# A scaled copy of 16,384 tokens for two experts each: the later weights move from SyncE's DMA queue to ScalarE's

## The chip, the cores and the metric

The kernel runs on one NeuronCore of a Trainium2 chip. Time is the device time of one execution in microseconds (us). VectorE (DVE in the profile) and ScalarE (ACT) compute; SyncE (SP) and ScalarE issue the DMA transfers, each to a queue of its own (q1 for SyncE, q10 for ScalarE), and 16 DMA engines of the core carry them out. TensorE and GpSimd take no part in the work.

## What is computed

```python
x               # 16 x 1024 x 512, float32
expert_weights  # 16 x 1024 x 2, float32
x_expanded = x[:, :, np.newaxis, :].repeat(2, axis=2)
weights = expert_weights[..., np.newaxis]
return (x_expanded * weights).astype(np.float32)
```

Each token's row of 512 numbers is written twice, once times each of its two weights. 33.6 MB are read and 67.1 MB are written. The indices of the experts are not used.

## The kernel before

The 16,384 tokens are 128 partitions times 128 tokens. They are cut into five tiles of 25 tokens on every partition (`groups`) and a rest of 3 (`LAST`). In each tile a partition's tokens lie next to each other in memory, so a load or a store moves one run of bytes for each partition: 25 tokens of x are a run of 51,200 bytes.

Three kinds of buffers stand in on-chip memory. `w_tile` holds all weights. `x_pool` has two buffers for a tile's x, so that tile i + 2 can be loaded when tile i has been used (line 164). `o_ring` holds the products of one tile, 25 tokens of 1,024 numbers, and every tile writes into the same places; the place of a piece is free again when its store has landed. The last 3 tokens have a small buffer of their own for x, `z_tile`.

A tile is worked on in pieces (`CUTS`): tile 0 in tokens 0 to 2, 2 to 13 and 13 to 25, the others in 0 to 13 and 13 to 25. `fill` (line 145) gives the first tokens of a piece to VectorE, in instructions of up to 4 tokens (line 130), and the others to ScalarE, one instruction of 512 numbers for each token and weight (line 120). After each piece `emit` has SyncE issue its store (line 155). The text calls the store of tile i's piece j "store i.j".

The loads of x are issued by ScalarE (line 80), tile 0's in three steps of 2, 7 and 16 tokens (`FIRST`). Loading tile 2 also brings the last tokens' x (line 87); a copy of one element (line 77) goes ahead of it.

The weights are issued by SyncE. Tile 0's are issued right after the first step of its load (line 85). The others come in three transfers, `later_weights` (line 101): tiles 1 and 2, tiles 3 and 4, and the last 3 tokens. The first two have, for each partition and tile, a run of 50 numbers, 200 bytes; the third a run of 24 bytes. They are issued once store 0.0 has been (line 157). What puts them there is the copy of line 102, a VectorE copy from `o_ring` into the part of `w_tile` that they fill: it comes after the first product, and the transfers have to come after it.

Each engine carries out its own instructions in their order, and so does each queue. The order between engines is kept by semaphores that the framework adds. An engine that issues transfers also waits at times, before an issue, for an earlier transfer that counts on the same semaphore.

Of the kernel before, what the change touches and what calls it, by code (L numbers as in the profile page):

```python
# [1 line left out]

# [4 lines left out]


@with_exitstack
def kernel(  # L10
    ctx: ExitStack,
    tc: tile.TileContext,
    x: bass.AP,
    expert_indices: bass.AP,
    expert_weights: bass.AP,
    out: bass.AP,
):
    nc = tc.nc

    batch, seq, hidden = x.shape  # L20
    k = expert_weights.shape[-1]
    P = nc.NUM_PARTITIONS
    ntok = batch * seq
    assert ntok % P == 0
    A_TOTAL = ntok // P

    f32 = mybir.dt.float32
    row = k * hidden
    CH = 4


    groups = [25, 25, 25, 25, 25]
    TX = max(groups)
    LAST = 3
    FIRST = [2, 7, 16]
    CUTS = [[0, 2, 13, 25], [0, 13, 25]]
    SHARES = [[2, 7, 9], [8, 8]]
    assert sum(groups) + LAST == A_TOTAL

    xf = x.rearrange("b s h -> (b s) h")  # L40
    of = out.rearrange("b s k h -> (b s) (k h)")
    wf = expert_weights.rearrange("b s k -> (b s) k")

    w_pool = ctx.enter_context(tc.tile_pool(name="w_pool", bufs=1))
    x_pool = ctx.enter_context(tc.tile_pool(name="x_pool", bufs=2))
    o_pool = ctx.enter_context(tc.tile_pool(name="o_pool", bufs=1))

    w_tile = w_pool.tile([P, A_TOTAL * k], f32)
    o_ring = o_pool.tile([P, TX * row], f32)

    def rows(of_all, done, T):
        return of_all[done * P : (done + T) * P, :].rearrange(
            "(p a) n -> p (a n)", a=T
        )


    if LAST:
        z_pool = ctx.enter_context(tc.tile_pool(name="z_pool", bufs=1))
        z_tile = z_pool.tile([P, LAST * hidden], f32)

    tiles = []
    done = 0
    for n in groups:
        tiles.append((done, n))
        done += n

    loaded = []

    def load(i):
        if i >= len(tiles):  # L70
            return
        done, n = tiles[i]
        x_tile = x_pool.tile([P, TX * hidden], f32)
        src = rows(xf, done, n)
        steps = FIRST if i == 0 else [n]
        if i == 2 and LAST:
            nc.scalar.copy(out=z_tile[:, :1], in_=o_ring[:, TX * row - 1 :])  # L77
        for e, step in enumerate(steps):
            at = sum(steps[:e])
            nc.scalar.dma_start(  # L80
                out=x_tile[:, at * hidden : (at + step) * hidden],
                in_=src[:, at * hidden : (at + step) * hidden],
            )
            if i == 0 and e == 0:
                weights(0, T0)
        if i == 2 and LAST:
            nc.scalar.dma_start(out=z_tile, in_=rows(xf, A_TOTAL - LAST, LAST))
        loaded.append(x_tile)


    T0 = groups[0]
    head = len(tiles) * T0

    def weights(at, to):
        g = (to - at) // T0
        nc.sync.dma_start(
            out=w_tile[:, at * k : to * k].rearrange("p (g n) -> p g n", g=g),
            in_=wf[at * P : to * P, :].rearrange("(g p a) n -> p g (a n)", g=g, p=P),
        )

    def later_weights():
        nc.vector.tensor_copy(  # L102
            out=w_tile[:, T0 * k :], in_=o_ring[:, : (A_TOTAL - T0) * k]
        )
        weights(T0, 3 * T0)
        weights(3 * T0, head)
        nc.sync.dma_start(
            out=w_tile[:, head * k :], in_=rows(wf, head, A_TOTAL - head)
        )

    def product(engine, o_tile, t, x_in, c, m):

        o = t * row
        if engine is not None:
            for e in range(m * k):
                out_e = o_tile[:, o + e * hidden : o + (e + 1) * hidden]
                in_e = x_in[:, e // k * hidden : (e // k + 1) * hidden]
                w_e = w_tile[:, c + e : c + e + 1]
                if engine is nc.scalar or engine is nc.any and (c + e) % 3 == 2:
                    nc.scalar.mul(out=out_e, in_=in_e, mul=w_e)  # L120
                else:
                    nc.vector.tensor_scalar(
                        out=out_e,
                        in0=in_e,
                        scalar1=w_e,
                        scalar2=None,
                        op0=mybir.AluOpType.mult,
                    )
            return
        nc.vector.tensor_tensor(  # L130
            out=o_tile[:, o : o + m * row].rearrange(
                "p (t k h) -> p t k h", t=m, k=k
            ),
            in0=x_in[:, : m * hidden]
            .rearrange("p (t h) -> p t h", t=m)
            .unsqueeze(2)
            .to_broadcast([P, m, k, hidden]),
            in1=w_tile[:, c : c + m * k]
            .rearrange("p (t k) -> p t k", t=m)
            .unsqueeze(3)  # L140
            .to_broadcast([P, m, k, hidden]),
            op=mybir.AluOpType.mult,
        )

    def fill(o_tile, x_in, c, m, v):
        for t in range(0, v, CH):
            u = min(t + CH, v)
            product(None, o_tile, t, x_in[:, t * hidden : u * hidden], c + t * k, u - t)
        product(nc.scalar, o_tile, v, x_in[:, v * hidden :], c + v * k, m - v)

    def emit(src, dst, c, cuts, shares):
        for at, to, v in zip(cuts, cuts[1:], shares):
            o_tile = o_ring[:, at * row : to * row]
            fill(o_tile, src[:, at * hidden : to * hidden], c + at * k, to - at, v)
            nc.sync.dma_start(out=dst[:, at * row : to * row], in_=o_tile)  # L155
            if c == 0 and at == 0:
                later_weights()

    for i in range(2):
        load(i)  # L160
    for i, (done, n) in enumerate(tiles):
        form = min(i, 1)
        emit(loaded[i], rows(of, done, n), done * k, CUTS[form], SHARES[form])
        load(i + 2)
    emit(
        z_tile,
        rows(of, A_TOTAL - LAST, LAST),
        (A_TOTAL - LAST) * k,
        [0, LAST],
        [LAST],  # L170
    )

# [1 line left out]
_INS = ['x', 'expert_indices', 'expert_weights']  # L174
_OUTS = [((16, 1024, 2, 512), 'float32')]


# [23 lines left out]
```

## Time and profile before

| | |
|---|---|
| median of 3 runs | 240.14 us (239.68 to 240.2) |
| the profiled execution, its time | 239.99 us |
| its span in the profile | 238.2 us |
| VectorE busy | 93.6 us, 24 instructions |
| ScalarE busy | 55.1 us, 88 instructions |
| moved by the DMA engines | 100.80 MB, 423 GB/s over the span |

In the profile's rows L130 is line 130 of the kernel; "out<-in" names the buffer that is written and the one that is read; x3 is a count of instructions. SPq and ACTq are the issues of DMAs by SyncE and ScalarE. A row of the timeline has the start and the time from the first to the end of the last of its instructions, in us, and in brackets how long the engine was idle before it and what ended that. A row of DMA issues has the size of one transfer and the us from its issue to its landing. A row of a DMA queue has the number of its packets, MB, and the time that they took as a share of 16 engines' time in the stretch. A row of stretches has the stretch in us from the start and its length, the busy us of VectorE, ScalarE and GpSimd with their instructions, the clock, the DMA engines' share and their GB/s. The line of digits divides the span into 40 slices of about 6 us; 9 is a share of 90% or more.

### The profile page before, as it was taken

The page shows a single profiled execution, that of the slowest core. Times are in us where ns is not written, and L with a number is a line of the kernel's source. Part 1 is how long each engine was busy: PE and PEld are TensorE (multiplying, and loading weights), DVE is VectorE, ACT ScalarE, POOL GpSimd, SP SyncE. Part 2 cuts the span into 40 slices and gives each one's busy share as a digit, 9 for nine tenths or more (in the row PEclk, how much of TensorE's full clock was granted, in tenths as well). Part 3 has the DMA queues.
Part 4 walks back from the last instruction along what each step waited for, and adds up shares of the span by engine and source line. Part 5 has one row for each costly group of instructions (what it writes and reads, how often), then busy time and mean ns, then how long its engine had stood idle before and what let it go on. Part 6 is the DMA issues. An engine that isn't in the chain of part 4 may idle for free.

```text
span 238.2 us, 213 instructions
## 1 busy us (share of the span) xinstructions
DVE 93.6 (39%) x24; ACT 55.1 (23%) x88; POOL 0.2 (0%) x4
## 2 busy tenths in 40 slices
DVE  2774910000068292095005902910085292861300
ACT  0004920000063260090005202700080280800000
POOL 0000000000000000000000000000000000000000
DMA  7999999998999999999999999999999999999996
GB/s 261 423 437 435 414 466 484 432 378 386 484 396 396 532 438 425 424 404 406 403 484 443 447 433 416 405 412 473 447 429 438 416 396 486 429 429 444 413 398 262
DMA packets 3713, 100.80 MB, mean 423 GB/s; under 512 B 1152, under 2 KB 1152, under 8 KB 1408
## 3 DMA queue, kind: packets, MB, share of 16 engines
q1 hardware_dynamic: 2560, 67.24, 65.4%
q10 hardware_dynamic: 1152, 33.55, 33.2%
q14 instruction: 1, 0.01, 0.0%
HBM read 33.69 MB, written 67.11 MB: 423 GB/s over the span
## 4 chain that ended last, share of the span: by engine, by line
DMA 53%; issue 20%; DVE 17%; ACT 3%; ACTq 0%; DVEq 0%; SPq 0%
DMA out_dram<-o_ring 45%; DVE o_ring L130 17%; DMA x_tile<-in_x_dram 8%; ACT o_ring L120 2%; ACT L120 1%; ACTq L80 0%; DVEq L130 0%; SPq L155 0%; ACTq L120 0%
## 5 line engine op out<-in xcount | busy, mean ns | idle before, releaser
L130 DVE TENSOR_TENSOR o_ring<-x_tile,w_tile 128x4096 f32<-128x4096 f32 (+3 forms) x22 | 90.0, 4131 | 122.1 <-DMA out_dram<-o_ring 64.0
L120 ACT ACTIVATE o_ring<-x_tile,w_tile 128x512 f32<-128x512 f32 x86 | 53.7, 708 | 132.5 <-DMA out_dram<-o_ring 132.5
L120 ACT ACT_TABLE_LOAD x1 | 1.3, 1283 | 20.9 <-DMA x_tile<-in_x_dram 20.9
L130 DVE TENSOR_TENSOR o_ring<-z_tile,w_tile 128x3072 f32<-128x3072 f32 x1 | 3.4, 3360 | 7.0 <-DMA out_dram<-o_ring 7.0
L102 DVE COPY w_tile<-o_ring 128x206 f32<-128x206 f32 x1 | 0.3, 269 | 0.0
L77 ACT COPY z_tile<-o_ring 128x1 f32<-128x1 f32 x1 | 0.2, 192 | 0.0
L185 POOL MEMSET const-bfloat16-1.0<- 128x1 bf16 x1 | 0.1, 102 | 0.0
L185 POOL MEMSET const-uint8-127<- 128x1 uint8 x1 | 0.1, 102 | 0.0
L185 POOL MEMSET const-float32-0.0<- 128x1 f32 x1 | 0.1, 99 | 0.2 <-issue 0.2
L185 POOL MEMSET const-float32-1.0<- 128x1 f32 x1 | 0.1, 99 | 0.0
## 6 DMA issues: line engine op xcount, KB each, us to landing
out_dram<-o_ring SPq DMA_DIRECT2D x5, 6144.0 KB, 36.7
out_dram<-o_ring SPq DMA_DIRECT2D x4, 6656.0 KB, 29.0
x_tile<-in_x_dram ACTq DMA_DIRECT2D x4, 6400.0 KB, 33.1
out_dram<-o_ring SPq DMA_DIRECT2D x1, 5632.0 KB, 40.2
x_tile<-in_x_dram ACTq DMA_DIRECT2D x1, 4096.0 KB, 19.2
x_tile<-in_x_dram ACTq DMA_DIRECT2D x1, 1792.0 KB, 7.8
out_dram<-o_ring SPq DMA_DIRECT2D x1, 1536.0 KB, 14.6
out_dram<-o_ring SPq DMA_DIRECT2D x1, 1024.0 KB, 17.9
```

Source lines behind the costliest of these rows:

```text
L77: nc.scalar.copy(out=z_tile[:, :1], in_=o_ring[:, TX * row - 1 :])
L102: nc.vector.tensor_copy(out=w_tile[:, T0 * k :], in_=o_ring[:, : (A_TOTAL - T0) * k])
L120: nc.scalar.mul(out=out_e, in_=in_e, mul=w_e)
L130: nc.vector.tensor_tensor(out=o_tile[:, o : o + m * row].rearrange("p (t k h) -> p t k h", t=m, k=k), in0=x_in[:, : m * hidden] .rearrange ...
L185: nc = _bacc.Bacc("TRN2", target_bir_lowering=False, num_devices=1)
```

## The change

The issuing engine becomes an argument of `weights`. `later_weights` is called while tile 0 is loaded, after its three steps and before the load of tile 1, and its three transfers are issued by ScalarE. The copy into `w_tile` is gone, and with it the call after store 0.0. On ScalarE the three issues stand between the third load of tile 0 and the load of tile 1; on SyncE store 0.1 follows store 0.0 directly. The waits of all other instructions name the same semaphores as before.

```diff
--- before.py
+++ after.py
@@ -82,7 +82,9 @@
                 in_=src[:, at * hidden : (at + step) * hidden],
             )
             if i == 0 and e == 0:
-                weights(0, T0)
+                weights(nc.sync, 0, T0)
+        if i == 0:
+            later_weights()
         if i == 2 and LAST:
             nc.scalar.dma_start(out=z_tile, in_=rows(xf, A_TOTAL - LAST, LAST))
         loaded.append(x_tile)
@@ -91,20 +93,17 @@
     T0 = groups[0]
     head = len(tiles) * T0
 
-    def weights(at, to):
+    def weights(engine, at, to):
         g = (to - at) // T0
-        nc.sync.dma_start(
+        engine.dma_start(
             out=w_tile[:, at * k : to * k].rearrange("p (g n) -> p g n", g=g),
             in_=wf[at * P : to * P, :].rearrange("(g p a) n -> p g (a n)", g=g, p=P),
         )
 
     def later_weights():
-        nc.vector.tensor_copy(
-            out=w_tile[:, T0 * k :], in_=o_ring[:, : (A_TOTAL - T0) * k]
-        )
-        weights(T0, 3 * T0)
-        weights(3 * T0, head)
-        nc.sync.dma_start(
+        weights(nc.scalar, T0, 3 * T0)
+        weights(nc.scalar, 3 * T0, head)
+        nc.scalar.dma_start(
             out=w_tile[:, head * k :], in_=rows(wf, head, A_TOTAL - head)
         )
 
@@ -153,8 +152,6 @@
             o_tile = o_ring[:, at * row : to * row]
             fill(o_tile, src[:, at * hidden : to * hidden], c + at * k, to - at, v)
             nc.sync.dma_start(out=dst[:, at * row : to * row], in_=o_tile)
-            if c == 0 and at == 0:
-                later_weights()
 
     for i in range(2):
         load(i)
```

## The prediction

> **What bounds the kernel now.** I read the page first, then the chain that ended last, then the timeline of the first 100 us, and last the DMA queues in single stretches. Three parts of the page say the same thing:
>
> ```profile
> span 238.2 us, 213 instructions
> DVE 93.6 (39%) x24; ACT 55.1 (23%) x88; POOL 0.2 (0%) x4
> DMA  7999999998999999999999999999999999999996
> ...
> q1 hardware_dynamic: 2560, 67.24, 65.4%
> q10 hardware_dynamic: 1152, 33.55, 33.2%
> ```
>
> No compute engine is busy for half of the span, and the 16 DMA engines are at 80% or more in all slices but the first and the last. q1 carries SyncE's transfers (all stores, all weights), q10 ScalarE's (all x). Together their packets take 98.6% of the span, 0.986 x 238.2 = 234.9 us of each DMA engine. So 3.3 us are all the idle time there is. The chain shows where some of it lies:
>
> ```profile
> 1.65 19.21 DMA x_tile<-in_x_dram
> ...
> 198.00 21.23 DMA out_dram<-o_ring
> ...
> 219.35 3.36 DVE o_ring L130
> ```
>
> Data first moves at 1.65 us. The last product ends at 219.35 + 3.36 = 222.71, and its store, in the issue rows below, lands 14.6 us later, at 237.3; 0.9 us of the span follow. Take 1.65 and 0.9 from 3.3, and 0.75 us of DMA idle time is left, ramps at both ends among it. That is the hard fact of this case: a reordering of transfers can win no more than this, plus what it makes the packets themselves cheaper.
>
> Now the stretch that the change touches:
>
> ```profile
> out_dram<-o_ring SPq DMA_DIRECT2D x1, 5632.0 KB, 40.2
> x_tile<-in_x_dram ACTq DMA_DIRECT2D x1, 512.0 KB, 3.9
> out_dram<-o_ring SPq DMA_DIRECT2D x1, 1536.0 KB, 14.6
> w_tile<-in_expert_weights_dram SPq DMA_DIRECT2D x2, 50.0 KB, 45.4
> w_tile<-in_expert_weights_dram SPq DMA_DIRECT2D x1, 25.0 KB, 2.7
> out_dram<-o_ring SPq DMA_DIRECT2D x1, 1024.0 KB, 17.9
> ```
>
> ```profile
> 0.72 4.30 ACTq L80 DMA_DIRECT2D x_tile<-in_x_dram  x4
> 7.02 0.27 DVE L102 COPY w_tile<-o_ring 128x206 f32<-128x206 f32 x1
> 7.41 1.02 SPq L96 DMA_DIRECT2D w_tile<-in_expert_weights_dram  x2
> 8.47 0.49 SPq L107 DMA_DIRECT2D w_tile<-in_expert_weights_dram  x1
> 8.96 7.69 DVE L130 TENSOR_TENSOR o_ring<-x_tile,w_tile 128x4096 f32<-128x4096 f32 x2 [1.68 <-DMA x_tile<-in_x_dram]
> 20.88 9.90 DVE L130 TENSOR_TENSOR o_ring<-x_tile,w_tile 128x4096 f32<-128x4096 f32 x3 [4.22 <-DMA x_tile<-in_x_dram]
> 27.27 4.02 SPq L155 DMA_DIRECT2D out_dram<-o_ring  x2
> 31.01 0.35 ACTq L80 DMA_DIRECT2D x_tile<-in_x_dram  x1
> 67.62 8.76 DVE L130 TENSOR_TENSOR o_ring<-x_tile,w_tile 128x4096 f32<-128x4096 f32 x2 [36.84 <-issue]
> 82.06 8.76 DVE L130 TENSOR_TENSOR o_ring<-x_tile,w_tile 128x4096 f32<-128x4096 f32 x2 [5.67 <-DMA out_dram<-o_ring]
> 90.90 0.36 ACTq L80 DMA_DIRECT2D x_tile<-in_x_dram  x1
> ```
>
> The later weights are issued from 7.41 and land some 45 us later, near 54. The second store (tile 0, tokens 2 to 13; I call it store 0.1) is issued at 27.27 behind them and lands at 27.27 + 40.2 = 67.5, when VectorE, after 36.84 us of waiting, may overwrite that part of the ring. The DMA queues of 22 to 50 us show why, and the two stretches after it what came of it:
>
> ```profile
> DMA packets 512, 12.37 MB, mean 442 GB/s; under 512 B 268, under 2 KB 268, under 8 KB 268
> q10 hardware_dynamic: 256, 12.29, 101.3%
> q1 hardware_dynamic: 256, 0.08, 1.1%
> ...
> DMA packets 628, 1.57 MB, mean 391 GB/s; under 512 B 484, under 2 KB 484, under 8 KB 612
> ...
> DMA packets 368, 16.58 MB, mean 436 GB/s; under 512 B 32, under 2 KB 32, under 8 KB 32
> ```
>
> 256 packets against 256: the two queues take turns packet by packet, and a 200-byte row of weights waits for a 51,200-byte row of x each time. The stores are indeed held. But the engines moved 442 GB/s meanwhile, nearly all of it x: tiles 1 and 2 were loaded ahead, and between 56 and 94 us (third row) the stores had the engines to themselves at 436. The hold changed the order of the bytes, not their rate. Only 50 to 54 us (second row), with 484 small packets, falls to 391: against the 439 around it a loss of 4 x (1 - 391/439) = 0.44 us.
>
> **The change, part by part.** The sum starts from the profiled execution's own 239.99 us; the median of the runs is 240.14.
>
> *The copy goes.* 0.27 us of VectorE at 7.02, in front of a product that then waited 1.68 us more for x. Cost and gain 0; without that cover 0.27.
>
> *Three issues leave SyncE's queue.* 1.02 + 0.49 = 1.51 us. The next instruction there is store 0.1, which isn't issued before 27.27 because ScalarE's products come late: 0. The Trainium skill speaks against more: "DMA: Bandwidth & Descriptors", section "Issuing engines are not separate DMA queues", has the DMAs of all issuing engines interleave on the same 16 DMA engines, so that another issuer saves sequencer time alone. By that rule the time stays 239.99; the 442 GB/s of the held stretch agree.
>
> *The same three issues enter ScalarE's queue* ahead of tile 1's load. The four loads' row reaches from 0.72 to 5.02, while the first load lands at 0.72 + 3.9 = 4.62, so I read the fourth issue as waiting for that landing. Three loads at about 0.4 us each end near 2, three weights near 3.5: inside that wait, 0. If the cover failed, tile 1's load would be queued 1.5 us later, near 6.2, still some 14 us before q10 has finished tile 0 at 20.88. ScalarE's products behind it wait for that landing too, so nothing behind it is held.
>
> *The rows of the weights change queue.* The three transfers make 256 + 256 + 128 rows, 48 small packets on each engine with the completions set aside. They now run in one go after tile 0's last load, from about 20.5 us, with the rest of the first store beside them. If the 0.44 us at 50 to 54 simply vanishes, -0.44. If every one of some 800 small packets pays what the 484 paid, 0.44 x 800/484 = 0.73, less the 0.44 already paid: +0.3. I take the middle, -0.1.
>
> *Loads and stores now mix.* Store 0.1, no longer held, takes turns with tiles 1 and 2. The smallest load took 3.9 us from issue to landing, so I allow some 3 to its first byte: it starts near 30. Tile 1's load has by then had 9 us at 442 GB/s, 4 MB; of the 13.1 MB of both tiles 9.1 remain, and some 8 MB of stores run beside them. Mixed stretches exist, tile 3's load at 96 to 124 us and tile 4's at 142 to 170, to be held against stores alone at 172 to 230:
>
> ```profile
> q1 hardware_dynamic: 140, 6.14, 50.7%
> q10 hardware_dynamic: 128, 5.94, 49.7%
> ...
> q1 hardware_dynamic: 140, 6.14, 50.6%
> q10 hardware_dynamic: 128, 5.99, 49.9%
> ...
> q1 hardware_dynamic: 554, 25.27, 100.6%
> ...
> 96.00:124.00 28.00, 8.76 (x2) 6.24 (x10) 0.00 (x0) 1.00 1.00 432
> 142.00:170.00 28.00, 8.76 (x2) 6.24 (x10) 0.00 (x0) 1.00 1.01 433
> 172.00:230.00 58.00, 29.64 (x7) 16.25 (x26) 0.00 (x0) 1.00 1.01 436
> ```
>
> Mixed, a MB takes 1.004 x 28 x 16 / 12.08 = 37.2 and 1.005 x 28 x 16 / 12.13 = 37.1 engine-microseconds; stores alone 1.006 x 58 x 16 / 25.27 = 36.9, x alone (22 to 50 us) 1.013 x 28 x 16 / 12.29 = 36.9. So mixing costs about 0.25 per MB: 17 MB x 0.25 / 16 = +0.27 us. By the rates in the last column (432.5 against 439) it would be 17 MB, 39.3 less 38.7 us, +0.6; but one row of 51,200 bytes on 16 engines is 0.8 MB, and a stretch's edge moves its rate by more than that difference. The low end is 0. I take +0.25.
>
> *Where the stall goes.* While alternating, store 0.1 has 45,056 of each 96,256 bytes, 47% of 432 = 203 GB/s: 5.77 MB take 28 us, landing near 58. VectorE starts tile 1 about 59 instead of 67.62 and issues its store near 68. In front of that store lies store 0.2, and when that lands the same bytes have moved as before (tile 0 to 2, weights, the first three stores, but for some rows of the last tokens): near 82 again. The next product starts where it started, at 82.06, tile 3's load at 90.90, and from there the old order repeats. So 8 us won at 59 become 14 us of slack (68 to 82) ahead of a full queue: 0 at the end. If a queue of stores ran dry here, each us of it would count fully.
>
> Sum: -0.1 + 0.25 = +0.15, 239.99 + 0.15 = **240.1 us**. With the ends -0.44 and +0.9 its own range is 239.6 to 240.9.
>
> **The rivals.** *Slower: the weights stand alone at the head of q10.* Near 21 us the first store is nearly through (issued after the first product, at 7.0, it landed 17.9 us later), and store 0.1 comes only at 27.27. If 48 small rows on each engine can't be streamed, nothing covers the gap before tile 1's rows. Its price goes up to one uncovered transfer: the first weights landed 2.7 us after their issue began, 0.37 of it issue time by the row below, so 2.3 us. It decides from about 0.5 us of gap. Halfway between the +0.3 above and 2.3 gives +1.3, 241.3 us.
>
> ```profile
> 0.73 0.37 SPq L96 DMA_DIRECT2D w_tile<-in_expert_weights_dram  x1
> ```
>
> For it: the dip at 50 to 54. Against it: 391 GB/s are no standstill, and x rows of tile 1 are queued right behind. The Trainium skill has a price for this: "DMA: Bandwidth & Descriptors", section "Measured (HBM→SBUF, 128 partitions, SWDGE, issued from GpSimd)", gives 0.95 us for 64 KB and 0.68 us for 4 KB, an estimate of 2.6 us for the three and 242.6 in all if none of it is covered; the trace's 0.44 us for most of these rows is far below it. Chance 0.28, a double price of mixing among it.
>
> *Faster: the earlier start reaches the end.* If the 0.75 us of unexplained idle time sit in the middle and vanish with the held stores, 239.2; with the whole 0.44 as well, 238.8. For it: tile 1 does start sooner. Against it: no slice between the second and the last but one is below 8 tenths. Chance 0.22.
>
> *The change doesn't do what it says:* stores could wait for x rows in turn whatever the weights do, store 0.1 landing near 67 again. Then the bytes are the same too, and the time is 240.0. 0.05, without a change of time.
>
> **How the numbers follow.** A measurement here tells 0.2%, about 0.48 us, from no change. The forecast has 0.45 and the ineffective change 0.05, both inside that: same 0.50, slower 0.28, faster 0.22. The range reaches to the slower rival's 241.3 and the faster one's 239.2, leaving their far ends out: 239.2 to 241.4.
>
> **What would show it.** Right: store 0.1 lands at 55 to 62 us instead of 67.5; VectorE's products at 82 and tile 3's load at 91 stay within 1 us; the DMA slices stay at 9; weights land near 22. Wrong: a slice at 20 to 30 us below 9 tenths (the slower rival); tile 3's load sooner than 89 (the faster one); a mean rate of 30 to 70 us below 430 GB/s (mixing dearer than taken).

## The result and the profile after

The changed kernel takes 240.93 us in the median of 22 runs (239.68 to 242.64), against 239.89 us (239.53 to 240.93) for the kernel before. The ratio is 1.005, with a 95% interval of 1.0036 to 1.0065: slower by some 1.1 us (1.04 between the medians, 1.2 by the ratio), where no change was the likeliest forecast. Two more samplings of 12 runs each gave 1.0044 (1.0017 to 1.0072) and 1.0045 (1.0028 to 1.0062). The runs also spread more widely than before. One execution further down, of e10, took 243.97 us and counts as a slow run, so that e10's ratio leaves it out.

From the page of the changed kernel, whose profiled execution took 241.64 us:

```profile
span 239.9 us, 212 instructions
DVE 93.3 (39%) x23; ACT 55.1 (23%) x88; POOL 0.2 (0%) x4
DMA  6999999999999999999999999999999999999983
...
q1 hardware_dynamic: 1872, 67.14, 64.8%
q10 hardware_dynamic: 1840, 33.66, 33.2%
...
out_dram<-o_ring SPq DMA_DIRECT2D x1, 5632.0 KB, 32.0
```

The rows of the moved weights are now in q10's count. The packets take 64.8 + 33.2 = 98.0% of the span, 0.980 x 239.9 = 235.1 us of each DMA engine: as much as before (234.9). No slice in the middle has a hole. What is new is the last slice, 3 tenths instead of 6, after one of 8. Here are the last microseconds in finer slices of 0.25 us, 230 to 240 us, first of before, then of after:

```profile
DMA  0499944017496969699996945110000000000000
GB/s 0 197 1376 393 786 197 197 0 49 295 197 492 295 590 295 541 295 492 442 393 541 295 541 197 246 49 49 0 0 0 0 0 0 0 0 0 0 0 0 0
```

```profile
DMA  9994490089989594969999432212020110000000
GB/s 393 1376 590 197 197 393 0 0 344 442 393 344 639 246 541 197 492 295 492 393 492 492 197 148 98 98 49 98 0 98 0 49 49 0 0 0 0 0 0 0
```

Both keep up the full rate to about 235.7 us. Before, the last data starts at 236.6. After, it goes on at 49 to 98 GB/s until 238.2, and 49 GB/s in a slice is one 12,288-byte row: a few engines, at the end one alone, still have work when the others have none. The timeline of after shows what the start of the changed region did, and where the time was lost:

```profile
2.12 1.54 ACTq L98 DMA_DIRECT2D w_tile<-in_expert_weights_dram  x2
3.70 0.50 ACTq L106 DMA_DIRECT2D w_tile<-in_expert_weights_dram  x1
4.96 0.35 ACTq L80 DMA_DIRECT2D x_tile<-in_x_dram  x1
...
59.85 8.76 DVE L129 TENSOR_TENSOR o_ring<-x_tile,w_tile 128x4096 f32<-128x4096 f32 x2 [28.71 <-issue]
...
81.46 8.76 DVE L129 TENSOR_TENSOR o_ring<-x_tile,w_tile 128x4096 f32<-128x4096 f32 x2 [12.85 <-DMA out_dram<-o_ring]
90.29 0.36 ACTq L80 DMA_DIRECT2D x_tile<-in_x_dram  x1
...
128.99 8.76 DVE L129 TENSOR_TENSOR o_ring<-x_tile,w_tile 128x4096 f32<-128x4096 f32 x2 [17.05 <-DMA out_dram<-o_ring]
...
175.08 8.76 DVE L129 TENSOR_TENSOR o_ring<-x_tile,w_tile 128x4096 f32<-128x4096 f32 x2 [17.84 <-DMA out_dram<-o_ring]
...
221.02 3.36 DVE L129 TENSOR_TENSOR o_ring<-z_tile,w_tile 128x3072 f32<-128x3072 f32 x1 [6.96 <-DMA out_dram<-o_ring]
```

The last four of the corresponding products stood in before at:

```profile
82.06 8.76 DVE L130 TENSOR_TENSOR o_ring<-x_tile,w_tile 128x4096 f32<-128x4096 f32 x2 [5.67 <-DMA out_dram<-o_ring]
...
127.83 8.76 DVE L130 TENSOR_TENSOR o_ring<-x_tile,w_tile 128x4096 f32<-128x4096 f32 x2 [17.55 <-DMA out_dram<-o_ring]
...
173.42 8.76 DVE L130 TENSOR_TENSOR o_ring<-x_tile,w_tile 128x4096 f32<-128x4096 f32 x2 [17.42 <-DMA out_dram<-o_ring]
...
219.35 3.36 DVE L130 TENSOR_TENSOR o_ring<-z_tile,w_tile 128x3072 f32<-128x3072 f32 x1 [6.97 <-DMA out_dram<-o_ring]
```

After is 0.60 us ahead at 82 us (some rows of the last tokens' x are still to come then), 1.16 behind at 129, 1.66 behind at 175, and 1.67 at the end. Each of these products waits for a store, and a store has landed when the slowest of the 16 engines has written its part. So the loss arises while tile 3's and tile 4's loads run beside the stores, 60 us and more behind the place of the change, and in single engines, since their mean did not move.

**One engine out of step.** The trace lists every DMA packet. It does not name the engine, but on one engine a row starts 3 to 4 ns ahead of the recorded end of the row before it, so that an engine can be followed row by row. The stretch in which store 0.1's first rows come in, of after first, then of its third sampling (e8 below); q10 carries x, q1 this store, with packets, MB and the packets' time as a share of the stretch on 16 engines:

```profile
DMA packets 16, 0.81 MB, mean 542 GB/s; under 512 B 0, under 2 KB 0, under 8 KB 0
q10 hardware_dynamic: 15, 0.77, 123.6%
q1 hardware_dynamic: 1, 0.05, 6.9%
```

The same stretch of the third sampling:

```profile
q10 hardware_dynamic: 15, 0.77, 147.9%
q1 hardware_dynamic: 1, 0.05, 6.9%
```

One turn of the 16 engines (30.4 to 31.9 and 30.1 to 31.6 us): 15 take a row of tile 1's x, and one takes the store's first row. From there that engine takes a store row when the others take x, and the other way round. In the second sampling (e2) it was 13 and 3. The store was issued at 27.2 to 27.6 and its rows were there some 3.4 us later, just while the engines were ending their rows of x (30.2 to 31.1): some ended a moment too early for the store, one or a few late enough. Then tile 3's load begins. The first rows of it that start after 95.2 us in after, and after 95.85 in e8:

```profile
q10 hardware_dynamic: 1, 0.05, 14.2%
```

```profile
q10 hardware_dynamic: 1, 0.05, 30.6%
```

One packet each, of 51,200 bytes on one engine, 0.142 x 16 x 1.4 us = 3.18 us and 0.306 x 16 x 0.75 = 3.67 us long, where such a row takes 1.89. The other 15 engines had begun theirs between 94.7 and 95.2, and this one came 0.6 to 0.7 us later. In e2 it took 2.6 us. Nothing behind that place levels it: from 172 us on, when there are only stores, the engines' distances stay the same within some 0.15 us.

Followed to the end, the engine out of step is the last one in e8: it finishes its rows at 238.7 us and the other 15 by 236.3. In e2 three engines finish at 236.6 to 237.4 and the others by 236.2. In the first profile of after, however, the engine with the row of 3.18 us finishes at 237.9 and is only the last but one. The last, at 238.7, had been in step near 30 us and near 95; it lost 2.6 us during tile 4's load, where its rows of x took 2.77, 2.11, 2.12, 2.50 and 2.59 us between 144 and 168 us. The first of them stands alone in the window of 144.275 to 144.3 us, 6.922 x 16 x 0.025 us long:

```profile
q10 hardware_dynamic: 1, 0.05, 692.2%
```

The product at 175 us waited for this engine, which finished that store's rows at 174.6 us, so the half microsecond that after loses between 129 and 175 us is its doing; being out of step at tile 1 does not explain it. In before, too, the last engine (lag 0.7 in the table below) had three rows of x of 2.2 to 2.3 us in the loads of tiles 3 and 4. So the loss is that of single engines in all three profiles of after, but not in each by the same step.

An accounting of the profiles bears out that the last engine sets the span. "Packets" is the sum of all packets' times divided by 16; "lag" is how far the last engine's completion of the last store is behind the mean of the 16; both are worked out from the trace's records.

| profile | span | packets | lag | rest |
|---|---|---|---|---|
| before | 238.2 | 235.2 | 0.7 | 2.2 |
| e1, before again | 238.2 | 235.1 | 0.9 | 2.2 |
| after | 239.9 | 235.1 | 2.4 | 2.3 |
| e2, after again | 238.5 | 235.2 | 1.2 | 2.2 |
| e8, after again | 239.8 | 235.1 | 2.5 | 2.2 |
| e12, store 0.1 0.7 us sooner | 237.6 | 234.9 | 0.3 | 2.4 |

In these rows the rest stays within 0.2 us, and the difference in span between the first and the third row, 1.7 us, is the difference in lag.

### The profile page after: what moved, and what is told of

The parts are those of the page before. It is cut to its first block, busy times and chain, and to the rows that moved or that the text cites. A ratio compares the mean times of both kernels' runs of the same rounds, so it can differ in the third digit from the quotient of the medians.

```text
span 239.9 us, 212 instructions
## 1 busy us (share of the span) xinstructions
DVE 93.3 (39%) x23; ACT 55.1 (23%) x88; POOL 0.2 (0%) x4
## 2 busy tenths in 40 slices
DMA packets 3713, 100.80 MB, mean 420 GB/s; under 512 B 1152, under 2 KB 1152, under 8 KB 1408
## 3 DMA queue, kind: packets, MB, share of 16 engines
q1 hardware_dynamic: 1872, 67.14, 64.8%
q10 hardware_dynamic: 1840, 33.66, 33.2%
## 4 chain that ended last, share of the span: by engine, by line
DMA 57%; issue 17%; DVE 17%; ACT 3%; ACTq 0%; DVEq 0%; SPq 0%
DMA out_dram<-o_ring 49%; DVE o_ring L129 17%; DMA x_tile<-in_x_dram 8%; ACT o_ring L119 2%; ACT L119 1%; ACTq L80 0%; DVEq L129 0%; SPq L154 0%; ACTq L119 0%
```

## The experiments

Thirteen runs were made, each timed in five rounds against the kernel before. The expectations call the theories by letters, which came up in this order: S, the spread of the engines at the end, arising from order; N, one bad draw; A, the weights' issues on ScalarE's queue; F, the freed stores as such; L, a load that joins the stores while all engines stand in step; O, one engine out of step.

**Is it repeatable? (e1, e2, e8: the two kernels unchanged)**

> The kernel before once more, as the measure of what repeats. All theories: ratio 1.000 +- 0.002. Theory S (spread of the DMA engines at the end): its profile again has the DMA engines running out within about 1.2 us of each other at the end (before: the share falls from 236.0 and is gone at 237.0), and its times stay within 239.5 to 241. Theory N (the profile of after shows one bad draw that either kernel could have had): its tail would be now and then as long as after's 3 us, its runs spread as widely as after's 239.7 to 242.6.

> The changed kernel once more. S: ratio 1.004 to 1.007 (about 241), runs spread over 2 to 3 us, the tail of the profile longer than 1.2 us whenever its run is above 240.5. N: 1.000 to 1.003 with a tail like before's. Theory A (ScalarE's issues of the weights near 2 us delay the start): the first product starts at 4.9 to 5.0 again instead of 4.69.

> The changed kernel a third time, for a third profile of the spread: F and L both want span = 2.3 us + mean packet time of an engine + how far the last engine is behind the mean, within 0.2 us, whatever the draw; ratio 1.003 to 1.007.

e1: 1.0004 (0.9987 to 1.0021). e2: 1.0044, its first product at 4.29 us, sooner than before's 4.69, so that the late start in the first profile of after (4.96) was a draw and A loses its first half. e8: 1.0045. N falls: the loss came three times out of three, while its size varies within a kernel's runs (e2's went from 239.09 to 242.37), as the accounting has it.

**The stores freed in two other ways (e3, e5)**

```diff
-        if i == 0:
+        if i == 1:
             later_weights()
```

> The weights stay on ScalarE's queue, but are issued after tile 1's load: the start is as in before (ScalarE issues nothing but x until 4.6 us), while the stores are free as in after. S: nothing gained, 1.003 to 1.007 (about 241). A: 1.000 to 1.002 (240.0), first product at 4.7, weights near 36 us without harm.

e3: median 240.18, ratio 1.0036 (1.0019 to 1.0053); S has it in its band, and A wanted 1.002 at most. The lag was 0.2 us, but the packets took 235.8 us. Its rows of x took 2.6 to 2.9 us instead of 1.89 on all 16 engines at the one turn, near 30 us, at which store 0.1 joined, about 0.8 us of each engine. The weights, now behind tile 1's x, landed so late that tile 1's products waited for them until 65.8 us. What that cost is not separated out; rows of x between 76 and 80 us were longer, too, by 0.3 us of each engine.

```diff
-        weights(nc.scalar, T0, 3 * T0)
-        weights(nc.scalar, 3 * T0, head)
-        nc.scalar.dma_start(
+        weights(nc.gpsimd, T0, 3 * T0)
+        weights(nc.gpsimd, 3 * T0, head)
+        nc.gpsimd.dma_start(
```

> The three later weight transfers go to GpSimd's own queue: the stores are as free as in after, and ScalarE's queue is as in before. Theory F (the freed stores, taking turns with tiles 1 and 2, cost the time, in row times or in one late DMA engine): 1.002 to 1.006, tile 1's products near 60 us. Theory A (ScalarE's queue costs it): 1.000 to 1.001.

e5: median 240.07, 1.0020 (1.0001 to 1.0038), lag 0.7. Tile 1's products began at 60.2 as expected. The stores are just as free here and the loss is less than half of after's. So free stores alone are not the whole of it, and neither F nor A has the number to itself. In e3 and e5 all 16 engines met store 0.1 at the same turn, and in e5, too, the rows of x at that turn took 2.6 to 2.8 us. But e5 is not only the same transfers on another queue: GpSimd's moved the weights in fewer and larger packets (its page has 528 packets under 512 bytes, after's 1,152), which by the trace's records saved 0.3 us of each engine. Part of its smaller loss can be that.

**The stores held again (e4, e6, e7)**

```diff
+            nc.vector.scalar_tensor_tensor(
+                out=one, in0=x_next[:, :1], scalar=0.0, in1=one,
+                op0=mybir.AluOpType.mult, op1=mybir.AluOpType.add,
+            )
...
+                nc.sync.dma_start(
+                    out=dst[:, at * row : to * row], in_=o_ring[:, at * row : to * row]
+                )
```

> Weights on ScalarE's queue as in after, but stores 0.1 and 0.2 are held until tile 2's x has landed (two products of one element each that add 0 times an element of that x to the piece), so that loads and stores run one after the other as in before. S: back to before's time, 0.999 to 1.002 (up to 0.5 us of it a gap between the last load and the held store), tail within 1.2 us, runs within 1.5 us. A: stays at after's 1.004 to 1.006.

e4: 241.9 us (6 runs), 1.0096 (1.0081 to 1.0112): slower than either kernel, against S. Up to 82 us it was even ahead (81.74 where before has 82.06); the loss lies in the packets, 236.7 us, at tile 3's load. The DMA queues of e4 between 92.8 and 93.2 us, and of before between 92.5 and 94.5, one store row on each engine:

```profile
q1 hardware_dynamic: 16, 0.85, 670.8%
```

```profile
q1 hardware_dynamic: 16, 0.85, 98.3%
```

The same 16 rows of 53,248 bytes took 6.708 x 0.4 x 16 / 16 = 2.68 us each in e4 and 0.983 x 2 x 16 / 16 = 1.97 in before. In e4 the engines had come within 0.2 us of each other (before: 0.55), perhaps because the held stores were issued when the loads had just run out. That made theory L, and e7 was to test it:

```diff
+            nc.scalar.dma_start(
+                out=x_next[:8, 4096:12288],
+                in_=rows(xf, *tiles[2])[:8, 4096:12288],
+            )
```

> The held kernel of the first four once more, with 32 KB of tile 2's x loaded a second time on 8 of the 128 partitions, behind the last tokens' x: it puts some of the DMA engines about 1.2 us behind the others before tile 3's load starts. Theory L (a load that joins the stores while all engines stand in step makes the rows of all engines longer; in the held kernel the engines stood within 0.2 us of each other at 81 us and tile 3's load cost 1.9 us of each): rows of tile 3's load and the store beside it near nominal again, 240.3 to 241.0 although 0.6 to 1.2 us of work are added on those engines. If step has nothing to do with it: 242.5 to 243.1.

e7: 244.43 us (5 runs), 1.0193 (1.0171 to 1.0215). The added rows took far longer than reckoned (about 3.5 us each, not 1.2) and put half of the engines 2.5 us and more behind. By the trace's records the rows around the start of tile 3's load were 1.9 us over nominal on each engine in e4 and 0.8 us in e7, which goes the way of L, but the time says nothing clean. L stays open.

```diff
+        nc.vector.tensor_copy(out=spare, in_=o_ring[:, : 4 * T0 * k])
+        nc.sync.dma_start(
+            out=spare.rearrange("p (g n) -> p g n", g=4),
+            in_=wf[T0 * P : head * P, :].rearrange("(g p a) n -> p g (a n)", g=4, p=P),
+        )
```

> After, with the hold put back as it was: 512 rows of weights are also read into an unused buffer from SyncE's queue, behind store 0.0 and a copy, in one transfer. The real weights stay on ScalarE's queue. The extra rows are 32 on each engine, about 0.4 to 0.5 us of engine time. F: tile 1's products at 67 again, time 240.0 to 240.6 (1.000 to 1.003), runs within 1.5 us, no long tail. A, or that ScalarE's burst of weights is what does it: 241 or more (1.005 and up), before's loss plus 0.5. The last tokens' x is issued late here, near 52 us, which either theory prices at nothing.

e6 missed its aim: nothing was held, and tile 1's products began at 58.28 us. The small rows of the spare weights took turns with the small rows of the real ones and were through by 21.5 us. What a queue holds depends on what it takes turns with. Median 240.53, 1.0050 (1.0022 to 1.0078), with 0.4 us of it in the added packets; its profile had all engines in step and a lag of 0.6, its runs reached 243.15. It decides nothing.

**The meeting of store 0.1 and tile 1's rows, moved (e9 to e13)**

Theory O makes a sharp forecast: the weights may stay where the change put them and the stores free, if only store 0.1 comes at another moment of the engines' turn.

```diff
-    SHARES = [[2, 7, 9], [8, 8]]
+    SHARES = [[2, 6, 9], [8, 8]]    # e9 (on after) and e11 (on before)
+    SHARES = [[2, 8, 9], [8, 8]]    # e10 (on after)
```

> After, with one token of piece 0.1 moved from VectorE to ScalarE: two more products of 0.71 us there, so store 0.1 is issued 1.41 us later; against the 1.89 us of a row of x that is a shift of the meeting by -0.48 us. Theory O (one engine out of step: when store 0.1 meets tile 1's rows near 30 us, a single DMA engine takes its turns the other way round than the other 15; it then takes the first row of tile 3 alone, near 95.7 us, and that row lasted 3.2, 2.6 and 3.7 us instead of 1.89 in the three profiles of after; it stays behind to the end): the engines meet in step, no row over 2.5 us near 96, the last engine less than 1.2 us behind the mean, 240.0 to 240.4 (1.000 to 1.0025). If the freed stores cost it in any case, through mixing or row times: 1.004 to 1.006 as after.

> After, with one token more of piece 0.1 on VectorE: store 0.1 is issued 1.41 us sooner, a shift of the meeting by +0.48 us within a row. O: as in the later one, 1.000 to 1.0025, unless the shift puts another engine on the other side, in which case a profile shows that engine out of step and the time is after's. Otherwise: 1.004 to 1.006.

> Control: the same token moved in the kernel before, whose stores wait for the weights anyway. O and the others: no change, 0.999 to 1.001. If moving the token is worth something by itself, it shows here.

e9: median 239.66, 1.0011 (0.9988 to 1.0035). e10: 239.71, 1.0000 (0.9979 to 1.0020). e11: 239.78, 0.9995 (0.9981 to 1.0009). O has its numbers, with a lag of 0.4 us in both profiles, though single runs still reached 242.16 and 241.55 us, and the control shows that the token itself is worth nothing. One thing in the expectations was wrong: the store did not come later in e9. The token that went to ScalarE has its x in tile 0's second step, so that ScalarE loads its table and starts before the third step is there. Store 0.1 was issued at 25.95 in e9 and at 26.02 in e10, both some 1.6 us sooner than in after. So the two are one experiment, made twice. The next two move it by one product only:

```diff
-                if engine is nc.scalar or engine is nc.any and (c + e) % 3 == 2:
+                if engine is nc.scalar and c + e != 13 * k - 1:
```

> After, with one single product of 128x512 (the last of piece 0.1) moved from ScalarE to VectorE, so that store 0.1 is issued 0.7 us sooner, at 26.6 to 26.9. In the profiles so far its rows are there some 3.4 us after the issue: in after that fell among the ends of the engines' rows of x (30.2 to 31.1 us), here it falls ahead of them. O: all 16 DMA engines take the store's first row at the same turn, no row over 2.5 us at 96, time 239.6 to 240.3 (0.999 to 1.002). Freed stores as such: 1.004 to 1.006.

e12: median 239.76, 1.0011 (0.9997 to 1.0026); the kernel before had 239.77 beside it. Its issue of store 0.1 (27.17 to 27.62 in the three profiles of after), its turn of 30.4 to 31.9 us, and tile 3's rows that start between 95.2 and 96.6:

```profile
26.90 0.33 SPq L154 DMA_DIRECT2D out_dram<-o_ring  x1
```

```profile
DMA packets 16, 0.72 MB, mean 481 GB/s; under 512 B 0, under 2 KB 0, under 8 KB 0
q1 hardware_dynamic: 16, 0.72, 111.9%
...
DMA packets 3, 0.15 MB, mean 110 GB/s; under 512 B 0, under 2 KB 0, under 8 KB 0
q10 hardware_dynamic: 3, 0.15, 25.3%
```

All 16 engines take the store in one turn, and the rows near 95 us are 0.253 x 16 x 1.4 / 3 = 1.89 us long. Its tail, in the slices of 230 to 240 us:

```profile
DMA  0999000054969898999989550000000000000000
```

The engines run out together at 236.0, where after's still worked at 238.2.

> The same edit in the kernel with the weights on GpSimd's queue, which had all engines in step (rows of x ending at 30.15 to 30.58 us, the store's rows there at about 31.1). 0.7 us sooner they are there at about 30.4, in the middle of those ends. O: the engines split here, some out of step; a row over 2.5 us near 96 on an engine, the last engine 1.2 us or more behind the mean in the profile, times spread over 2 us and more, 1.003 to 1.007. If being out of step isn't what costs: as without the edit, 1.000 to 1.003, or faster.

e13: median 240.39, 1.0027 (1.0013 to 1.0042). Its turn of 30.0 to 31.9 us, and the latest of tile 3's first rows, between 95.8 and 95.95:

```profile
q10 hardware_dynamic: 15, 0.77, 130.3%
q1 hardware_dynamic: 1, 0.05, 5.5%
```

```profile
q10 hardware_dynamic: 1, 0.05, 101.3%
```

In its profile one engine is out of step and finishes last, and its row took 1.013 x 16 x 0.15 = 2.43 us, just short of the 2.5 that O asked for. The lag was 1.0 us against e5's 0.7. But tile 0's last step landed 0.55 us later here than in e5's profile (VectorE goes on at 21.89 against 21.34 us), so that store 0.1 was issued at 27.66 us where e5 had 27.72: that the shift split the engines is not shown. The time went the way of O (240.07 to 240.39), but the two intervals overlap, so the opposite direction is not shown by the times.

## Why the prediction was wrong

*The bound and its reading.* That the DMA engines bound the kernel and that a reordering moves nothing in their total was right: 234.9 and 235.1 us. The step that failed is the one behind it, "Where the stall goes", which ended at 0 "from there the old order repeats". It reckoned with the 16 engines as one queue. Their order among each other did not repeat: in each of the three profiles of after, one to three came out of the meeting with store 0.1 in opposite turns, and one of these got a row of 3.2, 2.6 or 3.7 us at tile 3's load; in the first profile another engine lost 2.6 us at tile 4's; and nothing behind evened that out. The 0.75 us of idle time bounded what a reordering can win; nothing in the working bounded what it can lose at the end, where only the last engine counts. The term that stood at 0 has a size now: a lag of 0.7 to 0.9 us in the two profiles of before, 1.2 to 2.5 in those of after, and 0.3 in e12, where store 0.1 was issued one product sooner and the loss was gone.

*The copy, the three issues on SyncE and on ScalarE: 0.* Right. ScalarE's three end near 4.2 us, and tile 1's load is issued at 4.96, upon the first load's landing.

*The rows of the weights, -0.1.* Nearly right: by the trace's records the later weights' rows took 0.58 us of each engine in both kernels. And the slower rival with its gap near 21 us is out: in after the stretch of 20 to 22 us has more than the full rate.

```profile
20.00:22.00 2.00, 0.76 (x1) 0.71 (x1) 0.00 (x0) 1.00 1.55 585
```

*Mixing, +0.25.* As a mean over engines the total did not rise. The trace's records show two sums that cancel: store 0.1's joining costs 0.1 to 0.5 us on each engine, and the last tokens' rows, which before had shared the weights' last rush at 51 to 53 us at a price of 0.3, now take their nominal time. Mixed stretches were not dearer in general; one turn was, the first. The sign that the prediction had set for dearer mixing, under 430 GB/s from 30 to 70 us, did come by a hair, with 428 GB/s in after:

```profile
30.00:70.00 40.00, 9.90 (x4) 7.70 (x14) 0.00 (x0) 1.00 0.99 428
```

But before had 423 in the same stretch, so that 430 divided nothing.

*The course of the stores* was right: store 0.1 landed at 27.62 + 32.0 = 59.6 us (forecast 55 to 62), the products at 82 and tile 3's load at 91 within 1 us. With slices at 9 and the weights in by about 22 us, all its signs of being right came, and the loss arose where none of them looked: behind 91 us, in single engines.

*The rivals.* The slower one had the right sign, but its gap near 21 us did not occur. That the measured 240.93 us lies inside the stated range, which had been drawn out to this rival's 241.3, is therefore luck. The faster one fell: tile 1 did start 7.8 us sooner, and none of it reached the end. That the ineffective change was excluded follows from 59.6. The Trainium skill, "DMA: Bandwidth & Descriptors", section "Why a DMA increments its semaphore by 16 and not by 1", has a transfer run on up to 16 engines that finish independently, and only the full count says that it has landed. Read beside the last slices of before, where the engines already ended 1 us apart, that would have been a reason to ask what the change does to the last engine, and not only to the mean.

*What stays open:* that the moment of the meeting decides over the loss is shown by e9, e10 and e12. That it does so through the engine out of step is read from the profiles of e2 and e8; the first profile of after has it only in part, and e13 did not show the opposite direction. Why a row that starts 0.6 us behind the other 15 takes 2.6 to 3.7 us, why an engine in step lost 2.6 us at tile 4's load, and why rows of all 16 engines grow when a store joins loads, no run here told apart.

## What to carry to other kernels

When 16 DMA engines are full from end to end, the kernel ends with the last of them. Moving a transfer to another queue leaves the bytes as they were, but changes at which moment of the engines' turn two streams meet; in the profiles here a split there put one to three engines out of step, and what single engines lost at the loads behind it stayed until the end. Look at the last microseconds in fine slices, sample the profile more than once, and try a shift of the later stream by a fraction of a row (here one product of 0.7 us was enough) before you call a reordering good or bad.

## What was not expected of the hardware

Two queues take turns row by row, whatever the rows' sizes: 256 against 256 in before, 51,200 bytes against 200. The Trainium skill, "DMA: Bandwidth & Descriptors", section "Queues, rings and completion order", lets an engine drain a packet of 9 to 17 descriptors before it switches; here it switched after each row. Small rows by themselves are cheap: in after the 640 rows of the three transfers lie between 20.3 and 21.7 us, ahead of tile 1. And the turn in which a second stream joins the first can cost some 0.7 to 1 us of each engine, as in e3 (2.6 to 2.9 us for rows of 1.89) and in e4 at tile 3's load (2.68 for rows of 1.97).
